# A fourth paired slab in every gate and up group, with hidden tiles split by adding DMAs

## The chip, the cores and the metric

The kernel runs on one core of one Trainium2 chip. The metric is device microseconds from the start to the end of one execution. The median of three runs of the kernel before is 1436.71 us (1436.64 to 1439.13).

The engines are called by their names in the profile: PE multiplies matrices and accumulates into PSUM banks, ACT (ScalarE) casts and applies functions, DVE (VectorE) adds and subtracts, POOL (GpSimd) here issues DMAs of its own queue, SP issues the weight loads.

## The reference

One layer over 256 rows of width 2048: four mixers side by side, a cross attention, and a SwiGLU of width 5632, each behind a norm, with residual sums. All is float32. The part that matters here:

```python
def swiglu(h, w_gate_up, w_down):
    gate, up = jnp.split(h @ w_gate_up, 2, axis=-1)
    return (jax.nn.silu(gate) * up) @ w_down
...
        x = x + swiglu(rms_norm(x, norm_g[l, 2]), w_gate_up[l], w_down[l])
    return rms_norm(x, final_norm_g)
```

## The kernel before

**Two parts per operand.** Every operand of a matrix product is split into a high part, rounded to the short float32 form that PE multiplies in one pass (`fp32r`), and a low part, what the rounding left. A product is three matmuls: high by high, high by low, low by high (`part`, lines 431 to 436). ACT casts the high part of a weight (`wh`), DVE subtracts it from the original to get the low part (`wl`), and PE can multiply by a piece of weight only when both are there.

**The weight stream.** All weights come in the order of use as slabs of 16 blocks of 128x128, 1 MB each, into one of three buffers `raw`. A slab is prepared in halves of up to 1024 columns (`_half`, lines 132 to 138: cast at 135, subtraction at 136). Four pairs of buffers hold prepared halves; `_fill` writes the preparation of a half three halves ahead of its use. A half's cast has to wait until PE has finished with the half four places earlier.

**Ordinary and paired slabs.** In the gate and up product each of ten groups makes 512 columns of gate and 512 of up for both row blocks of 128. Its work is a plan of eight letters, one per slab. An ordinary slab, "N", holds four pieces of 512 columns, each multiplied for two row blocks: 24 matmuls. A paired slab, "S", holds two pieces of gate and two of up for two of the 16 inner tiles; by sums of weights and sums of activations (`combine`, lines 438 to 455, made once, kept in tiles `z`) the same product takes seven parts and not eight: 21 matmuls (`paired_rows`, lines 491 to 505). Its weights are prepared in four halves of 1024, 512, 1024 and 1024 columns (`_sums`, lines 140 to 165: adds at 157, casts at 159, subtractions at 160), which PE uses for 6, 3, 6 and 6 matmuls. The sums overwrite the raw columns: the first add writes columns that the first half reads.

The sums of weights are made in two ways. In a slab of the set `SUMMED` a tile `two` gets a copy of one quarter twice by SP and then two other quarters added on top by an adding DMA on POOL's queue (`_load`, lines 98 to 106); DVE then adds twice. In the other paired slabs, those of the down product, DVE adds four times. `two` has two buffers, and its DMAs are issued when the slab before is loaded.

**The end of a group.** After the third paired slab, `mixed` (line 1064) makes the mixed sums from four PSUM banks with four adds on DVE, `gated` (1073) adds the gate banks and takes the Silu on ACT, and after the eighth slab `upped` (1079) adds the up banks, multiplies by the row gains and the gate, transposes and sends the hidden tiles to memory with two DMAs of POOL.

**Hidden tiles.** The hidden values return turned, as 44 tiles of 128x256 (`fetch`, lines 1087 to 1103): a POOL DMA loads a tile into a temporary, then `split` (289) casts its high part on ACT and subtracts its low part on DVE into a slot `f`. The first 22 come back during the groups, the others at the start of the down product, which reads `f` in two passes.

**Order.** A scheduler orders each engine's instructions from the program, by order of writing among those that are ready in its own reckoning of time; each engine then executes its list in that order. `keep_place` (line 309) ties instructions to their written place. Background work (`Background`) is written between matmuls by due times reckoned from PE's and DVE's work.

Of the kernel before, what the change touches and what calls it, by code (L numbers as in the profile page):

```python
# [13 lines left out]
F32 = mybir.dt.float32  # L14
F32R = mybir.dt.float32r
# [4 lines left out]
ALU = mybir.AluOpType  # L20
# [3 lines left out]
P = 128  # L24
R = 256
D = 2048
KT = D // P
DFF = 5632
# [13 lines left out]
LATE = 12  # L42

GATE_UP = 1920 // 16 + 8
GROUP = "NNSNSNSN"

DOWN = GATE_UP + 80
PASSES = "NNNNSNNSNNSNNSNNSNNSNN", "NSNSNSNSNSNSNSNSNSNNNN"

PAIRED = {a + i for a, plan in [(GATE_UP + 8 * j, GROUP) for j in range(10)] + [(DOWN, PASSES[0]), (DOWN + 22, PASSES[1])]  # L50
          for i, x in enumerate(plan) if x == "S"}
SUMMED = {i for i in PAIRED if i < DOWN}

LAG, OWED, SOON, FAR = 1.3, 0.9, 0.01, 18.0
V_NG = 0
# [16 lines left out]
class Stream:  # L72
# [21 lines left out]
    def _load(self, n):  # L94

        nc = self.nc
        self.raw = self.rawp.tile([P, 2048], F32, name="raw", tag="raw")
        if n // 16 + 1 in SUMMED:
            W, t = self.W[n // 16 + 1], self.sums.tile([P, 1024], F32, name="two", tag="two")
            for a in (0, 512):  # L100
                nc.sync.dma_start(t[:, a:a + 512], W[:, 1536:2048])
            nc.gpsimd.dma_start(t, W[:, 512:1536], accum_op=ALU.add)  # L102
            self.two.append(t)
        if n // 16 in SUMMED:
            nc.sync.dma_start(self.raw[:, 0:1536], self.W[n // 16][:, 0:1536])
            return
        for a, b in zip(CUTS[n], CUTS[n][1:]) if n in CUTS else [(0, 1024), (1024, 2048)] if self.after else [(0, 2048)]:
            (nc.scalar if (n, a) == (0, 0) else nc.sync).dma_start(self.raw[:, a:b], self.W[n // 16][:, a:b])
            if self.after:
                self.after.pop(0)()  # L110

    def _half(self):

        nc, n = self.nc, self.made
        if n % 16 == 0 and self.phase == 0:
            self._load(n)
        if n // 16 in PAIRED:
            return self._sums()
# [86 lines left out]
class Background:  # L205
# [17 lines left out]
    def first(self, g):  # L223

        self.q.sort(key=lambda e: e[0] is not g)
# [29 lines left out]
class Block:  # L255
# [42 lines left out]
    def split2(self, hi, lo, src):  # L298
        self.nc.scalar.copy(hi, src)
        self.tt(lo, src, hi.bitcast(F32), ALU.subtract)  # L300

    def gap(self, pool, n):

        pool.tile([P, n // 4], F32, name=f"gap{next(self.kept)}")
# [159 lines left out]
    def paired_rows(self, w, cols, slots, sums, plan, mixed, first, ready=None, late=0, before=None, swap=False):  # L464

        st, s, nk = self.st, len(sums), len(slots)  # L470
        rest = [k for k in range(nk) if not any(k in ks for ks, _ in sums)]
        steps = [(c, k) for c in range(2) for k in rest]
        todo, q = iter(sums), {}
        count = {"a0": len(rest) + s, "a1": len(rest) + s, "b0": len(rest) + s, "b1": len(rest)}
        left, total = {}, 0

        def put(name, hi, lo, wh, wl):
            if name not in q:
                for x in [name] if name in count else "1675":
                    q[x] = (self.bank if (name in count) == swap else self.gbank)()  # L480
                    left[x] = count.get(x, s)
            new = left[name] == count.get(name, s)
            left[name] -= 1
            self.part(q[name][:, :], hi, lo, wh, wl, new, left[name] == 0)

        form = lambda t, r: (t[:, r * P:(r + 1) * P], t[:, R + r * P:R + (r + 1) * P])
        n = done = 0
        for i, kind in enumerate(plan):
            if before:
                before(i)  # L490
            if kind == "S":
                ks, z = next(todo)
                a = [form(slots[ks[0]], 0), form(slots[ks[1]], 0), form(slots[ks[1]], 1)]
                hi, lo, x4 = self.forms(z, slots[ks[0]])
                x1, s2, s3 = ((hi[:, i * P:i * P + P], lo[:, i * P:i * P + P]) for i in range(3))
                t = (("5", x1), ("7", s3))
                pairs = iter((("1", a[0]), ("b0", x4), ("a0", a[1]), *(t if st.n // 16 in SUMMED else t[::-1]), ("a1", a[2]), ("6", s2)))
                for parts in st.take_sums(w, ks, cols):
                    for wh, wl in parts:
                        name, (hi, lo) = next(pairs)  # L500
                        put(name, hi, lo, wh, wl)
                        self.bg.poll()
                done += 1
# [543 lines left out]
    def gate_up(self, gp, f, z):  # L1047
# [39 lines left out]
        def fetch(k0, k1, ahead, pause, wait=0):  # L1087

            m = {}
            for k in range(k0, k1 + ahead):  # L1090
                if k < k1:
                    while len(stored) <= k // 4:
                        yield
                    m[k] = self.tmp()
                    self.load_turned(m[k], self.ff, k)
                if k >= k0 + ahead:
                    while wait and self.bg.now < stored[(k - ahead) // 4] + wait:
                        yield
                    mark = self.mark()
                    self.split(f[k - ahead], m.pop(k - ahead))  # L1100
                    self.keep_place(mark)
                    self.have = k - ahead + 1
                    yield pause

# [15 lines left out]
                yield 3.0  # L1120
                yield from self.combine(z, *(self.h3[k] for k in ks))

        sums = [((2 * i, 2 * i + 1), z[i]) for i in range(GROUP.count("S"))]
        comb = self.bg.add(combined())
        ps = self.gemm_rows("w_gate_up", [0, DFF], self.h3,
                            parts=[(range(8), [0]), (range(8, 12), [0]), (range(12), [1]), (range(12, 16), [0]), (range(12, 16), [1])],
# [4 lines left out]
        early = self.bg.add(fetch(0, FT - 22, 3, 2.0, 15))  # L1131
        self.bg.drain(comb)
        for j in range(1, DFF // 512):
            upped(j, self.paired_rows("w_gate_up", [j * 512, DFF + j * 512], self.h3, sums, GROUP, mixed, gated, swap=j % 2 == 0)[0])
        self.bg.drain(early)
        self.fetch = self.bg.add(fetch(FT - 22, FT, 6, SOON))

# [73 lines left out]
    def down_end(self, f, ss, ps, rest, split):  # L1211
# [6 lines left out]
        def norm(p, r):  # L1218

            s, y, b, v, a = ss[:, 4 * r + 3:4 * r + 4], *(ss[:, 8 + 4 * r + i:9 + 4 * r + i] for i in range(4))  # L1220
            if r == 0:
                self.tt(self.half(3, 0), self.half(3, 0), p, ALU.add)
                p = self.half(3, 0)
            nc.scalar.activation(self.bank()[:, :], p[:, :], AF.Square, accum_out=s)
            nc.scalar.activation(y, s, AF.Abs_reciprocal_sqrt, scale=1.0 / D, bias=b)
            nc.vector.scalar_tensor_tensor(out=v, in0=s, scalar=1.0 / D, in1=b, op0=ALU.mult, op1=ALU.add)

            nc.vector.scalar_tensor_tensor(out=a, in0=y, scalar=v, in1=y, op0=ALU.mult, op1=ALU.mult)
            nc.vector.scalar_tensor_tensor(out=v, in0=a, scalar=-10.0 / 3, in1=a, op0=ALU.add, op1=ALU.mult)
            nc.vector.scalar_tensor_tensor(out=a, in0=v, scalar=5.0, in1=y, op0=ALU.add, op1=ALU.mult)  # L1230
            for c in range(4):
                x = self.half(c, r)
                if c == 3:
                    nc.vector.scalar_tensor_tensor(out=x, in0=p[:, :], scalar=a, in1=fg[:, 3 * 512:4 * 512], op0=ALU.mult, op1=ALU.mult)
                elif c:
                    nc.scalar.activation(x, x, AF.Copy, scale=a)
                else:
                    nc.vector.tensor_scalar(out=x, in0=x, scalar1=a, scalar2=None, op0=ALU.mult)
                (nc.scalar if c == 1 else nc.sync).dma_start(self.t["out"][r * P:(r + 1) * P, c * 512:(c + 1) * 512], x)

        mark = self.mark()
# [7 lines left out]
        for r in range(2):  # L1249
# [4 lines left out]
            for c in range(3):  # L1254
                x = self.half(c, r)
                self.stt(x, x, 0.375, fg[:, c * 512:(c + 1) * 512], ALU.mult, ALU.mult)
        nc.scalar.mul(fg[:, 3 * 512:4 * 512], fg[:, 3 * 512:4 * 512], 0.375)
        for r in range(2):
            for k, wh, wl in held:
                self.part_rows(ps[r], r, f[k], wh, wl, False, k == FT - 1)  # L1260
            norm(ps[r], r)


# [627 lines left out]
```

## Time and profile before

The profiled execution took 1435.07 us, 1.64 us under the median; its span from first to last instruction is 1433.3 us.

| engine | busy us | share of the span |
|---|---|---|
| PE | 1423.0 | 99% |
| DVE | 1146.2 | 80% |
| ACT | 815.2 | 57% |
| POOL | 234.8 | 16% |

The ten gate and up groups with pairs run from about 778 to 1193 us of the span, the down product from there to the end. A row of the timeline gives start, duration, engine, line, operation, output and inputs, shapes, the count of instructions merged into the row, and in brackets the engine's idle time before it and what ended it. A row of stretches gives the length and then each engine's busy time.

### The profile page before, as it was taken

How to read it: one execution, taken by the hardware profiler on the slowest of the kernel's cores; microseconds unless marked ns; L12 is line 12 of the kernel's file. 1: busy time of each engine (PE TensorE's matmuls, PEld its weight loads, DVE VectorE, ACT ScalarE, POOL GpSimd, SP SyncE). 2: the span in 40 equal slices, each digit the busy share in tenths (PEclk: the TensorE clock that was granted, in tenths of full speed). 3: DMA queues.
4: the chain of work that ended last, by engine and by line, in shares of the span. 5: the costliest groups of instructions: out<-in, count | busy, mean ns of one | idle time of the engine just before them, and what ended most of it. 6: DMA issues, size and time to landing. Idle time of an engine off the chain costs nothing.

```text
span 1433.3 us, 18652 instructions
## 1 busy us (share of the span) xinstructions
PE 1423.0 (99%) x6589; PEld 1180.7 (82%) x6589; DVE 1146.2 (80%) x1738; ACT 815.2 (57%) x1183; POOL 234.8 (16%) x306
## 2 busy tenths in 40 slices
PE   9999999999999999999999999999999999999997
PEld 8888888888888888888888888888888888888886
DVE  6667868777877767777677888898888888989997
ACT  7556565446645555556554656555555556655655
POOL 0000100013212223531431121122011002000000
PEclk9999999999999999999999999999999999999999
DMA  9876564546667788964986999889999887655554
GB/s 352 299 285 248 205 206 162 175 169 224 202 196 236 234 267 252 274 200 166 289 239 209 286 286 277 278 275 282 294 293 288 268 260 229 219 230 179 193 218 147
DMA packets 73037, 343.79 MB, mean 240 GB/s; under 512 B 10957, under 2 KB 12654, under 8 KB 45168
## 3 DMA queue, kind: packets, MB, share of 16 engines
q1 hardware_dynamic: 54848, 288.98, 57.5%
q0 software_dynamic: 17664, 52.97, 15.8%
q8 instruction: 51, 0.84, 0.2%
q10 hardware_dynamic: 432, 0.66, 0.1%
q14 instruction: 42, 0.34, 0.1%
HBM read 322.12 MB, written 20.45 MB: 239 GB/s over the span
## 4 chain that ended last, share of the span: by engine, by line
PE 97%; DVE 1%; ACT 0%; DMA 0%; issue 0%; SPq 0%; ACTq 0%
PE pg L433 22%; PE pg L434 22%; PE pg L435 22%; PE pm L434 7%; PE pm L435 7%; PE pm L433 7%; PE pg L381 4%; PE pg L382 2%; PE pm L1344 1%; PE pm L1022 1%; PE pm L993 1%; DMA raw<-in_W 0%; PE pm L1753 0%; DVE res L283 0%; PE pm L994 0%
## 5 line engine op out<-in xcount | busy, mean ns | idle before, releaser
L136 DVE TENSOR_TENSOR wl<-raw,wh 128x1024 fp32r<-128x1024 f32 (+1 forms) x413 | 494.8, 1212 | 166.1 <-ACT wh L135 163.2
L135 ACT CAST wh<-raw 128x1024 fp32r<-128x1024 f32 (+1 forms) x413 | 424.5, 1043 | 283.9 <-PE pg L435 196.4
L433 PE MATMUL pg<-wh,act 128*128 128x512 f32 (+1 forms) x1191 | 465.6, 391 | 0.0
L434 PE MATMUL pg<-wl,act 128*128 128x512 f32 (+1 forms) x1191 | 463.9, 389 | 0.4 <-DVE wl L136 0.2
L435 PE MATMUL pg<-wh,act 128*128 128x512 f32 (+1 forms) x1191 | 463.9, 389 | 0.0
L433 PEld LDWEIGHTS pg<-wh,act 128*128 128x128 f32 x1191 | 223.8, 188 | 47.8 <-issue 1.5
L434 PEld LDWEIGHTS pg<-wl,act 128*128 128x128 f32 x1191 | 223.8, 188 | 47.2 <-DVE wl L136 1.3
L435 PEld LDWEIGHTS pg<-wh,act 128*128 128x128 f32 x1191 | 223.7, 188 | 47.2 <-DVE act L283 0.4
L159 ACT CAST wh<-raw 128x1024 fp32r<-128x1024 f32 (+1 forms) x150 | 137.0, 921 | 146.8 <-DVE raw L157 46.4
L160 DVE TENSOR_TENSOR wl<-raw,wh 128x1024 fp32r<-128x1024 f32 (+1 forms) x150 | 156.1, 1061 | 57.0 <-ACT wh L159 56.8
L434 PE MATMUL pm<-wl,act 128*128 128x512 f32 x309 | 120.5, 390 | 0.1
L433 PE MATMUL pm<-wh,act 128*128 128x512 f32 x309 | 120.2, 389 | 0.0
L435 PE MATMUL pm<-wh,act 128*128 128x512 f32 x309 | 120.2, 389 | 0.0
L381 PE MATMUL pg<-act,wh 128*128 128x512 f32 x256 | 90.5, 395 | 0.0
L382 PE MATMUL pg<-act,wl 128*128 128x256 f32 x256 | 71.8, 280 | 0.0
L434 PEld LDWEIGHTS pm<-wl,act 128*128 128x128 f32 x309 | 58.0, 188 | 13.0 <-DVE wl L136 0.6
L433 PEld LDWEIGHTS pm<-wh,act 128*128 128x128 f32 x309 | 58.0, 188 | 12.0
L435 PEld LDWEIGHTS pm<-wh,act 128*128 128x128 f32 x309 | 58.0, 188 | 12.0
L102 POOL DMA_DIRECT2D two<-in_W x30 | 26.6, 887 | 241.2 <-DMA two<-in_W 116.0
L157 DVE TENSOR_TENSOR raw<-raw 128x512 f32<-128x512 f32 x90 | 62.0, 689 | 1.3
L159 ACT CAST wh<-two 128x1024 fp32r<-128x1024 f32 x30 | 31.6, 1052 | 51.1 <-PE pg L435 21.7
L381 PEld LDWEIGHTS pg<-act,wh 128*128 128x128 f32 x256 | 48.1, 188 | 10.5
(375 smaller groups left out, 1821.9 us busy)
## 6 DMA issues: line engine op xcount, KB each, us to landing
raw<-in_W SPq DMA_DIRECT2D x216, 1024.0 KB, 5.6
raw<-in_W SPq DMA_DIRECT2D x30, 768.0 KB, 6.1
two<-in_W SPq DMA_DIRECT2D x60, 256.0 KB, 4.9
two<-in_W POOLq DMA_DIRECT2D x30, 512.0 KB, 9.3
raw<-in_W SPq DMA_DIRECT2D x11, 512.0 KB, 7.6
hidden<-g POOLq DMA_DIRECT2D x22, 256.0 KB, 3.7
tmp<-hidden POOLq DMA_DIRECT2D x44, 128.0 KB, 5.4
features<-tmp POOLq DMA_DIRECT2D x32, 128.0 KB, 5.3
```

Source lines behind the costliest of these rows:

```text
L102: nc.gpsimd.dma_start(t, W[:, 512:1536], accum_op=ALU.add)
L135: nc.scalar.copy(wh[:, a:b], r[:, a:b])
L136: nc.vector.tensor_tensor(out=wl[:, a:b], in0=r[:, a:b], in1=wh[:, a:b].bitcast(F32), op=ALU.subtract)
L157: nc.vector.tensor_tensor(out=out, in0=a, in1=b, op=ALU.add)
L159: nc.scalar.copy(wh, src)
L160: nc.vector.tensor_tensor(out=wl, in0=src, in1=wh.bitcast(F32), op=ALU.subtract)
L381: self.nc.tensor.matmul(p[:, :], wh, slot[:, :], start=start, stop=False)
L382: self.nc.tensor.matmul(p[:, 0:R], wl, slot[:, 0:R], start=False, stop=stop)
L433: self.nc.tensor.matmul(p, hi, wh, start=start, stop=False)
L434: self.nc.tensor.matmul(p, hi, wl, start=False, stop=False)
L435: self.nc.tensor.matmul(p, lo, wh, start=False, stop=stop)
L993: nc.tensor.matmul(p[:, :], q[d][:, r * P:(r + 1) * P], kt[d][:, :], start=d == 0, stop=False)
```

## The change

Four things change.

- The plan of a group is "NSNSsNSN" where it was "NNSNSNSN". The fourth paired slab, small "s", is not in `SUMMED`: it is loaded whole and DVE makes all its sums. A fourth combined tile `z3` lies in the pool of the group stage.
- The sums in `two` are loaded two slabs ahead of use where it was one.
- A hidden tile's low part is made in another way: ACT casts the tile a second time with factor -1 into the place of the low part, and an adding DMA on POOL's queue adds the tile to it. The two casts keep their written places.
- PE's matmuls of the paired plans, and those held for the last rows, keep their written places.

```diff
-GROUP = "NNSNSNSN"
+GROUPS = "NSNSsNSN",
...
-          for i, x in enumerate(plan) if x == "S"}
-SUMMED = {i for i in PAIRED if i < DOWN}
+          for i, x in enumerate(plan) if x in "Ss"}
+SUMMED = {GATE_UP + 8 * j + i for j in range(10) for i, x in enumerate(GROUPS[j % len(GROUPS)]) if x == "S"}
...
-        if n // 16 + 1 in SUMMED:
-            W, t = self.W[n // 16 + 1], self.sums.tile([P, 1024], F32, name="two", tag="two")
+        if n // 16 + 2 in SUMMED:
+            W, t = self.W[n // 16 + 2], self.sums.tile([P, 1024], F32, name="two", tag="two")
...
+    def split_far(self, hi, lo, src):
+
+        mark = self.mark()
+        self.nc.scalar.copy(hi, src)
+        self.nc.scalar.mul(lo, src, -1.0)
+        self.keep_place(mark)
+        self.nc.gpsimd.dma_start(lo, src, accum_op=ALU.add)
...
+            mark = self.mark()
             self.part(q[name][:, :], hi, lo, wh, wl, new, left[name] == 0)
+            self.keep_place(mark)
...
-            if kind == "S":
+            if kind in "Ss":
...
-                    mark = self.mark()
-                    self.split(f[k - ahead], m.pop(k - ahead))
-                    self.keep_place(mark)
+                    t = f[k - ahead]
+                    self.split_far(t[:, 0:R], t[:, R:512], m.pop(k - ahead))
...
-        sums = [((2 * i, 2 * i + 1), z[i]) for i in range(GROUP.count("S"))]
+        z = z + [gp.tile([P, 1024], F32R, name="z3")]
+        sums = [((2 * i, 2 * i + 1), z[i]) for i in range(4)]
...
-            upped(j, self.paired_rows("w_gate_up", [j * 512, DFF + j * 512], self.h3, sums, GROUP, mixed, gated, swap=j % 2 == 0)[0])
+            plan = GROUPS[(j - 1) % len(GROUPS)]
+            upped(j, self.paired_rows("w_gate_up", [j * 512, DFF + j * 512], self.h3, sums[:8 - plan.count("N")], plan, mixed, gated,
+                                      swap=j % 2 == 0)[0])
...
         for r in range(2):
+            mark = self.mark()
             for k, wh, wl in held:
                 self.part_rows(ps[r], r, f[k], wh, wl, False, k == FT - 1)
+            self.keep_place(mark)
             norm(ps[r], r)
```

More of the change, by code (lines that the diff above doesn't have):

```diff
@@ L44 @@
 GATE_UP = 1920 // 16 + 8
-GROUP = "NNSNSNSN"
+GROUPS = "NSNSsNSN",
 DOWN = GATE_UP + 80
 PASSES = "NNNNSNNSNNSNNSNNSNNSNN", "NSNSNSNSNSNSNSNSNSNNNN"
-PAIRED = {a + i for a, plan in [(GATE_UP + 8 * j, GROUP) for j in range(10)] + [(DOWN, PASSES[0]), (DOWN + 22, PASSES[1])]
-          for i, x in enumerate(plan) if x == "S"}
-SUMMED = {i for i in PAIRED if i < DOWN}
+PAIRED = {a + i for a, plan in [(GATE_UP + 8 * j, GROUPS[j % len(GROUPS)]) for j in range(10)] + [(DOWN, PASSES[0]), (DOWN + 22, PASSES[1])]
+          for i, x in enumerate(plan) if x in "Ss"}
+SUMMED = {GATE_UP + 8 * j + i for j in range(10) for i, x in enumerate(GROUPS[j % len(GROUPS)]) if x == "S"}
 LAG, OWED, SOON, FAR = 1.3, 0.9, 0.01, 18.0
```

## The prediction

> **What bounds the kernel now.** I read the page first: busy shares, then the slices. Then the busy time by stretches over the gate and up groups, the list of waits, and last the instructions in order of time around one group's end and one paired slab.
>
> ```profile
> span 1433.3 us, 18652 instructions
> PE 1423.0 (99%) x6589; PEld 1180.7 (82%) x6589; DVE 1146.2 (80%) x1738; ACT 815.2 (57%) x1183; POOL 234.8 (16%) x306
> DVE  6667868777877767777677888898888888989997
> ```
>
> TensorE (PE) is never free, so a matmul removed is worth its full time, provided nothing else then ends last. VectorE (DVE) is next: eight or nine tenths in the second half. The stretches (41 us is nearly one group):
>
> ```profile
> core 0: us, PE busy (x) PEld busy (x) DVE busy (x) ACT busy (x) POOL busy (x), PEclk, DMA share, GB/s
> 906.00:947.00 41.00, 40.94 (x180) 33.42 (x179) 36.10 (x45) 23.61 (x29) 7.76 (x9) 1.00 0.90 282
> 1111.00:1152.00 41.00, 41.00 (x182) 33.80 (x181) 35.40 (x41) 23.83 (x28) 4.21 (x5) 1.00 0.90 276
> 1300.00:1400.00 100.00, 100.00 (x443) 82.81 (x442) 96.09 (x138) 58.03 (x74) 0.00 (x0) 1.00 0.56 203
> 1400.00:1433.00 33.00, 24.54 (x108) 19.55 (x106) 23.85 (x50) 15.86 (x29) 0.00 (x0) 0.94 0.45 159
> ```
>
> DVE has 5 to 6 us left in 41. That rest is not free to use: it falls where DVE waits for ScalarE (ACT), which waits until PE gives a weight buffer back.
>
> ```profile
> PE pg L434 <- DVE wl L136: 0.2, 1, 0.2
> ...
> DVE wl L160 <- ACT wh L159: 50.5, 49, 1.7
> ```
>
> PE lost 0.2 us to weights in the whole run; DVE waited 50.5 us in the groups. The cause is the depth of four weight buffers (a "half" each: 12 matmuls in an ordinary slab, but 6, 3, 6, 6 in a paired one). The last half of a paired slab can only be cast when PE frees the buffer four halves back.
>
> **The gain.** PE at the end of one group: paired slab, ordinary slab, next group.
>
> ```profile
> 975.38 0.39 PE L433 MATMUL pm<-wh,act 128*128 128x512 f32 x1
> ...
> 980.14 0.39 PE L433 MATMUL pg<-wh,act 128*128 128x512 f32 x1
> ...
> 985.58 0.39 PE L433 MATMUL pm<-wh,act 128*128 128x512 f32 x1
> ```
>
> A paired slab takes 980.14-975.38 = 4.76 us (21 matmuls), an ordinary one 985.58-980.14 = 5.44 (24): 0.227 us per matmul. One more pair saves 0.68 us per group, 6.8 us in ten.
>
> **What DVE gets for it.** An ordinary slab costs DVE two 128x1024 subtractions. The new "s" slab is not summed by DMA: three 128x1024, one 128x512 and four adds. All of these stand in the second down pass:
>
> ```profile
> 1371.14 1.82 DVE L160 TENSOR_TENSOR wl<-raw,wh 128x1024 fp32r<-128x1024 f32 x2
> 1372.88 2.87 DVE L157 TENSOR_TENSOR raw<-raw 128x512 f32<-128x512 f32 x4
> 1375.66 1.22 DVE L160 TENSOR_TENSOR wl<-raw,wh 128x1024 fp32r<-128x1024 f32 x1
> ```
>
> Start to start, the 1024 with the 512 takes 1.74 us (1.14 and 0.60) and the four adds 2.78. The s slab: 3x1.14+0.60+2.78 = 6.80 us, against PE's 4.76. The ordinary slab it replaces: 2.28. So DVE gets 4.52 us per group, and 35.4 of 41 becomes about 40 in a group of 40.9. Work alone would just fit; with the waits above it does not.
>
> **First place: s directly behind S.** Now the DVE rows around a group's end and the paired slabs after it:
>
> ```profile
> 1151.70 1.22 DVE L136 TENSOR_TENSOR wl<-raw,wh 128x1024 fp32r<-128x1024 f32 x1
> ...
> 1154.63 1.41 DVE L287 SCALAR_TENSOR_TENSOR h<-h,rc,g 128x512 f32<-128x512 f32 x2
> 1155.95 1.30 DVE L557 STREAM_TRANSPOSE g<-h 128x512 f32<-128x512 f32 x2
> 1157.17 1.19 DVE L136 TENSOR_TENSOR wl<-raw,wh 128x1024 fp32r<-128x1024 f32 x1
> 1158.28 1.82 DVE L160 TENSOR_TENSOR wl<-raw,wh 128x1024 fp32r<-128x1024 f32 x2
> 1160.01 0.69 DVE L157 TENSOR_TENSOR raw<-two,raw 128x512 f32<-128x512 f32 x1
> 1161.09 1.23 DVE L160 TENSOR_TENSOR wl<-two,wh 128x1024 fp32r<-128x1024 f32 x1 [0.39 <-ACT wh L159]
> 1162.23 0.68 DVE L157 TENSOR_TENSOR raw<-raw 128x512 f32<-128x512 f32 x1
> 1164.11 1.23 DVE L160 TENSOR_TENSOR wl<-raw,wh 128x1024 fp32r<-128x1024 f32 x1 [1.19 <-ACT wh L159]
> ...
> 1174.01 1.23 DVE L160 TENSOR_TENSOR wl<-raw,wh 128x1024 fp32r<-128x1024 f32 x1 [1.54 <-ACT wh L159]
> 1175.37 2.36 DVE L136 TENSOR_TENSOR wl<-raw,wh 128x1024 fp32r<-128x1024 f32 x2
> ```
>
> ```profile
> 1172.93 1.05 ACT L159 CAST wh<-raw 128x1024 fp32r<-128x1024 f32 x1 [1.72 <-PE pm L435]
> 1174.29 2.00 ACT L135 CAST wh<-raw 128x1024 fp32r<-128x1024 f32 x2 [0.31 <-PE pm L435]
> ```
>
> ```profile
> 1177.44 0.39 PE L433 MATMUL pm<-wh,act 128*128 128x512 f32 x1
> ```
>
> At 1174.01 DVE subtracts the last half of a paired slab, at 1175.37 the first half of the next slab, both just after their casts, which waited for PE: neither can be earlier. PE reaches that next slab at 1177.44. Put s there. Its first add overwrites raw columns that its first half still reads, so no add can go ahead of 1175.37. DVE: first half to 1176.51, second to 1177.11, adds to 1179.89, third half done 1181.12 (1.23 long). PE wants it one matmul into the third half: 1177.44+9x0.227+0.23 = 1179.71. Late by 1.41. The fourth half's cast runs beside, its subtraction is done about 1182.3, wanted at 1181.07+1.41: no more. So 1.4 us in each of ten groups, 14.1.
>
> **Second place: the first pair one slab after the group's end.** DVE's end-of-group work (adds, gains, transposes) ran without a gap until 1157.17. PE began the new group at
>
> ```profile
> 1151.60 0.39 PE L433 MATMUL pm<-wh,act 128*128 128x512 f32 x1
> ```
>
> so 5.57 us later. Today the second ordinary slab covers this. After, PE reaches the paired slab at 1157.04 and its halves at 1158.40, 1159.08 and 1160.45. The piece at 1151.70 becomes that slab's first half. Behind 1157.17 come its second half (0.60), one add (0.60), the half from "two" (1.14) and the other add, the order these rows show when "two" is ready. Third half done: 1157.17+1.20+1.23 = 1159.60, wanted 1159.31, late 0.3. Other add done 1157.17+2.34+0.68 = 1160.19; cast 1.05, subtraction 1.23 and two 0.05 handovers: 1162.57, wanted 1160.67: late 1.9 in all. With both adds ahead of "two" (a day in the other order) it is 1.0. I take 1.9, for the rows after a group's end have that order. Nine groups follow a paired one: 17.1; the first follows a group with four such rows only.
>
> **The other edits.**
> SwiGLU low parts: 22 subtractions leave DVE in the early groups and 22 in the first down pass. The stretch with these (36.10) and one without (35.40) both ran without PE waits, and neither place above holds one, so I credit 0; at best 0.33 us in a few places. ACT gets 44 more casts, 0.40 each, 17.6 us at 57% busy: hidden. POOL gets 44 more issues:
>
> ```profile
> L564 POOL DMA_DIRECT2D tmp<-hidden x44: 884/884/904, 785.9 to 1226.5; - x44
> ...
> two<-in_W POOLq DMA_DIRECT2D x30, 512.0 KB, 9.3
> ...
> values<-tmp POOLq DMA_DIRECT2D x16, 128.0 KB, 2.2
> ...
> 1223.46 0.88 POOL L564 DMA_DIRECT2D tmp<-hidden  x1 [7.27 <-DVE act L283]
> 1225.62 1.76 POOL L564 DMA_DIRECT2D tmp<-hidden  x2 [1.28 <-DVE act L283]
> ...
> 1193.08 0.39 PE L433 MATMUL pg<-wh,f 128*128 128x512 f32 x1
> ```
>
> An adding DMA of 128 KB has no row; a plain one lands in 2.2 us, an adding one four times its size in 9.3. Down starts at 1193.08; its last hidden tile is wanted seven ordinary and two paired slabs and three steps of 1.36 later: 1193.08+38.1+9.5+4.1 = 1244.8. Its load is out by 1227.4 and lands about 5.4 later; with two casts, one issue and 9.3 it is whole by 1244. Covered, but narrowly: 0, or up to 9.3 if the queue holds it up. On the same queue a weight add can stand behind four hidden adds (a load's 5.4 plus 0.9 each); issuing it two slabs ahead adds 4.8 to 5.4 of slack, so 0. SP issues no more than before and the s slab loads 1 MB as the slab it replaces did; the hidden adds put 0.5 MB per group on some 11.6 (41 us at 282 GB/s): 0. The fourth combination falls in the first group, where DVE idles: 0. Kept places fix an order and issue nothing.
>
> **Sum**, against this execution's 1435.07 us (span 1433.3): -6.8+14.1+17.1 = +24.4, that is 1459.5. The median of the three runs stands 1.6 higher, so **1461 us**. Its own range runs from 1.0 at each place (-6.8+10+9, 1447) to 1472, when order adds half a subtraction to each.
>
> **Rivals.**
> *Faster.* The stall at both places is nothing, since VectorE has caught up by then: 1435.07-6.8 = 1428 (1430 at the median). For it: the second down pass alternates ordinary and unsummed paired slabs with DVE at 96.09 of 100 and PE at 100.00. Against it: there an ordinary slab, with 3.2 us to spare on DVE, stands ahead of each. It decides if lateness stays under 0.36 us at each of 19 places. 0.09. *Within 0.2%:* 0.04.
> *One place only.* If the scheduler draws the group's first paired slab ahead of gains and transposes (2.5 us of DVE), only s stalls: 1435.07-6.8+14.1 = 1442. Against it: 1151 to 1157 shows the opposite. 0.14.
> *Larger stalls by order.* Where a half is late, a ready half of the next slab may be put ahead of it on DVE, 1.14 us each: 19x1.14 = 21.7 more, 1482. For it: adds and halves already swap places in the rows. 0.16.
> *Late hidden tiles:* 9.3 more, 1470. 0.04.
> *The clock falls.* In the last stretch PE idled 8.46 of 33 us and the granted clock was 0.94, 2 us lost. If every stop after a group's end cost that: nine more times 2, 1479. The Trainium skill ("TensorE: Matmul & The Clock Gate", "Why this matters for your kernels") says only idle gaps beyond about 3 us bring the half-rate clock back; by that rule my stops, at most 1.9, keep the clock and the sum stands. No run here yet shows stops of that length. 0.03.
> The forecast keeps 0.50.
>
> **Numbers.** A difference under 0.2% (2.9 us) can't be told from none here. Leaving out faster and same (0.13) and the upper tip of the order rival gives 1441 to 1479. Faster 0.09, same 0.04, slower 0.87.
>
> **What would show it.** PE's matmuls fall by 30. The waits should list PE behind "wl" L160 with some 20 to 35 us, where it had 0.2; in each group one pause in the third half of s and one in the third or fourth half of the first pair. Group starts should lie about 44 us apart, not 41.6. I am wrong if PE still waits for nothing, or if it waits for hidden tiles or for "raw".

## The result and the profile after

The changed kernel takes 1536.99 us (median of five runs, 1533.58 to 1539.28), the kernel before beside it 1436.64 (1435.42 to 1439.13): a ratio of 1.0697 with a 95% interval of 1.0678 to 1.0716, slower. The profiled execution has a span of 1535.0 us, 101.7 more than before. The page of the changed kernel (busy time, and two rows of the 40 slices):

```profile
span 1535.0 us, 18725 instructions
PE 1450.3 (94%) x6559; PEld 1179.3 (77%) x6559; DVE 1178.3 (77%) x1762; ACT 846.8 (55%) x1249; POOL 274.0 (18%) x350
PE   9999999999999999999999999999999947799997
PEclk9999999999999999999999999999999968999998
```

The 30 matmuls are gone (6589 before). TensorE now stops, and four fifths along (slice 33 of 40, from 1228 us), where the groups end, it is down to four tenths for a slice and its granted clock falls. What it waited for, from the list of waits (engine, line, released by: us in total, times, longest):

```profile
PE pg L443 <- DMA f<-tmp: 18.3, 2, 14.9
PE pm L442 <- DVE wl L160: 12.4, 15, 0.9
PE pg L442 <- DVE wl L160: 11.1, 14, 0.9
PE pg L443 <- DMA act<-tmp: 10.2, 6, 3.0
PE pg L441 <- ACT f L305: 7.3, 1, 7.3
PE pg L443 <- DMA z<-tmp: 4.4, 1, 4.4
PE pm L441 <- ACT wh L159: 2.9, 6, 0.6
```

Lines 441 to 443 are the three matmuls of `part`: high by high, high by low weights, low by high weights. L160 makes the low weights, L305 and L308 are the first cast and the adding DMA of `split_far`. So there are two main kinds of wait: for low weights (L442, 23.5 us), and for hidden tiles, which before had none: 32.9 us for their low parts (L443, "DMA f", "act" and "z") and one stop of 7.3 for a high part (L441, "ACT f L305"). By stretches (span; PE, PEld, DVE, ACT and POOL busy; granted clock, DMA share, GB/s):

```profile
906.00:947.00 41.00, 37.95 (x161) 29.61 (x160) 37.47 (x45) 22.05 (x25) 4.19 (x5) 1.00 0.81 241
1111.00:1152.00 41.00, 39.37 (x169) 31.30 (x168) 34.95 (x43) 20.91 (x23) 3.75 (x5) 1.00 0.83 257
1240.00:1280.00 40.00, 18.70 (x62) 13.80 (x62) 6.95 (x7) 16.98 (x39) 36.98 (x42) 0.67 0.94 195
1340.00:1440.00 100.00, 100.00 (x442) 82.64 (x441) 90.86 (x136) 56.60 (x75) 0.84 (x1) 1.00 0.54 194
```

In the groups TensorE is short by 1.6 to 3.1 us of 41; in the 40 us behind the last group it gets through 62 matmuls instead of some 176, while GpSimd (POOL), busy 4 of 41 in the groups, is busy 36.98 of 40. The second down pass is untouched.

Adding up every distance between two matmul starts beyond the usual 0.227 us (those of 0.03 us and more) gives 46.2 us between 790 and 1231 (the groups), 55.8 between 1231 and 1350 (the start of down) and 5.9 behind it (all of it at the end); before had 1.9 from 790 to its end. Less that and 6.8 for the removed matmuls it is the difference, but for some 3 us, mostly of smaller distances.

### The profile page after: what moved, and what is told of

It reads as the page before. It is cut to its first block, busy times and chain, and to the rows that moved or that the text cites. A ratio compares the mean times of both kernels' runs of the same rounds, so it can differ in the third digit from the quotient of the medians.

```text
span 1535.0 us, 18725 instructions
## 1 busy us (share of the span) xinstructions
PE 1450.3 (94%) x6559; PEld 1179.3 (77%) x6559; DVE 1178.3 (77%) x1762; ACT 846.8 (55%) x1249; POOL 274.0 (18%) x350
## 4 chain that ended last, share of the span: by engine, by line
PE 83%; DVE 7%; DMA 3%; ACT 3%; issue 2%; POOL 1%; SPq 0%; ACTq 0%; POOLq 0%
PE pg L442 19%; PE pg L443 19%; PE pg L441 18%; PE pm L442 6%; PE pm L443 6%; PE pm L441 5%; PE pg L389 4%; DVE wl L160 3%; PE pg L390 2%; DVE raw L157 2%; DVE wl L136 2%; DMA tmp<-hidden 1%; PE pm L1358 1%; DMA raw<-in_W 1%; ACT wh L135 1%
## 5 line engine op out<-in xcount | busy, mean ns | idle before, releaser
L136 DVE TENSOR_TENSOR wl<-raw,wh 128x1024 fp32r<-128x1024 f32 (+1 forms) x393 | 472.0, 1212 | 191.6 <-ACT wh L135 189.8
L135 ACT CAST wh<-raw 128x1024 fp32r<-128x1024 f32 (+1 forms) x393 | 405.8, 1042 | 273.5 <-PE pg L443 192.2
L443 PE MATMUL pg<-wh,act 128*128 128x512 f32 (+1 forms) x1166 | 456.1, 391 | 10.8 <-DMA act<-tmp 10.2
L442 PE MATMUL pg<-wl,act 128*128 128x512 f32 (+1 forms) x1166 | 456.2, 391 | 6.7 <-DVE wl L160 6.5
L441 PE MATMUL pg<-wh,act 128*128 128x512 f32 (+1 forms) x1166 | 457.3, 392 | 4.9 <-ACT act L299 2.4
L159 ACT CAST wh<-raw 128x1024 fp32r<-128x1024 f32 (+1 forms) x190 | 174.6, 924 | 190.2 <-PE pg L443 87.7
L443 PEld LDWEIGHTS pg<-wh,act 128*128 128x128 f32 x1166 | 219.2, 188 | 60.3 <-DMA act<-tmp 13.2
L442 PEld LDWEIGHTS pg<-wl,act 128*128 128x128 f32 x1166 | 219.5, 188 | 56.4 <-DVE wl L160 10.2
L441 PEld LDWEIGHTS pg<-wh,act 128*128 128x128 f32 x1166 | 219.5, 188 | 54.1 <-ACT wh L159 3.6
L160 DVE TENSOR_TENSOR wl<-raw,wh 128x1024 fp32r<-128x1024 f32 (+1 forms) x190 | 199.0, 1063 | 69.5 <-ACT wh L159 69.2
L442 PE MATMUL pm<-wl,act 128*128 128x512 f32 x284 | 112.7, 397 | 7.7 <-DVE wl L160 7.7
L441 PE MATMUL pm<-wh,act 128*128 128x512 f32 x284 | 112.1, 395 | 2.3 <-ACT wh L159 2.3
L443 PE MATMUL pm<-wh,act 128*128 128x512 f32 x284 | 111.6, 393 | 0.0
L157 DVE TENSOR_TENSOR raw<-raw 128x512 f32<-128x512 f32 x130 | 89.4, 687 | 2.5
L442 PEld LDWEIGHTS pm<-wl,act 128*128 128x128 f32 x284 | 53.9, 190 | 22.6 <-DVE wl L160 11.5
L441 PEld LDWEIGHTS pm<-wh,act 128*128 128x128 f32 x284 | 53.9, 190 | 15.7 <-ACT wh L159 4.5
L443 PEld LDWEIGHTS pm<-wh,act 128*128 128x128 f32 x284 | 53.9, 190 | 11.0
L574 POOL DMA_DIRECT2D tmp<-hidden x44 | 53.3, 1417 | 17.8 <-DMA act<-tmp 6.1
```

The lines of the kernel that those rows point to most:

```text
L135: nc.scalar.copy(wh[:, a:b], r[:, a:b])
L136: nc.vector.tensor_tensor(out=wl[:, a:b], in0=r[:, a:b], in1=wh[:, a:b].bitcast(F32), op=ALU.subtract)
L157: nc.vector.tensor_tensor(out=out, in0=a, in1=b, op=ALU.add)
L159: nc.scalar.copy(wh, src)
L160: nc.vector.tensor_tensor(out=wl, in0=src, in1=wh.bitcast(F32), op=ALU.subtract)
L441: self.nc.tensor.matmul(p, hi, wh, start=start, stop=False)
```

## The experiments

All times are medians; each batch is set against its own runs of the kernel before, 1435.8 to 1437.1, so differences across batches are good to about 1 us. All runs also combine the fourth pair of tiles. In short, with the ratio and its interval:

| run | what it is | us | ratio |
|---|---|---|---|
| two_ahead | before + weight adds two slabs ahead | 1437.0 | 1.0002 (0.9993 to 1.0011) |
| old_plan | + the kept places | 1443.8 | 1.0052 (1.0034 to 1.0070) |
| early_far | + adding DMAs for the 22 early tiles | 1452.7 | 1.0112 (1.0098 to 1.0126) |
| three_pairs | + adding DMAs for all 44 | 1474.2 | 1.0257 (1.0236 to 1.0277) |
| false_debt | + 6 us a group in the reckoning only | 1499.1 | 1.0436 (1.0421 to 1.0452) |
| best_four | before + adds two slabs ahead, fourth pair, early tiles not held back | 1465.5 | 1.0197 (1.0182 to 1.0212) |
| undebted_near | + the kept places | 1493.5 | 1.0393 (1.0378 to 1.0409) |
| subtracted | + early tiles held back by the reckoning | 1499.5 | 1.0440 (1.0425 to 1.0456) |
| the change | + adding DMAs for all 44 | 1537.0 | 1.0697 (1.0678 to 1.0716) |

The upper five keep the old plan NNSNSNSN, the lower four have the new one; within each part every row adds one thing to the row above it.

### The planner's debt

A step of the prediction took the first 22 hidden tiles to come back during the groups. They don't. GpSimd's rows of the changed kernel (start, length, line, what, and in brackets the idle time ahead and what ended it):

```profile
793.33 0.85 POOL L308 DMA_DIRECT2D act<-tmp  x1 [3.98 <-ACT act L306]
...
1234.32 0.85 POOL L308 DMA_DIRECT2D act<-tmp  x1 [31.36 <-ACT act L305]
...
1244.78 3.55 POOL L308 DMA_DIRECT2D f<-tmp  x2
```

One adding DMA at 793.33, the next at 1234.32. (Twelve loads are drawn ahead into the first three groups, at 785 to 880; eleven of these tiles then sit unsplit in the eleven `tmp` places.) The code says why: `poll` (lines 241 to 244) steps background work only while `owed`, the VectorE work that the planner has reckoned and TensorE has not yet worked off, is under 0.9. By its own formula (elements/960 + 0.155 an operation) a group owed 37.7 us before against 41.5 of TensorE; with the unsummed pair it owes 42.3 against 40.8. By this reckoning the debt grows by 1.5 us from group to group, and the early tiles wait until they are drained behind the last one.

```diff
 # undebted
-            if self.owed < OWED and self.now >= e[1]:
+            if (self.owed < OWED or e[0] is self.free) and self.now >= e[1]:
...
-            e[1] = self.now + self.owed + (w or LAG)
+            e[1] = self.now + (0.0 if e[0] is self.free else self.owed) + (w or LAG)
...
+        self.bg.free = early
 # subtracted
-                    self.split_far(t[:, 0:R], t[:, R:512], m.pop(k - ahead))
+                    mark = self.mark()
+                    self.split(t, m.pop(k - ahead))
+                    self.keep_place(mark)
 # three_pairs
-GROUPS = "NSNSsNSN",
+GROUPS = "NNSNSNSN",
 # false_debt: as three_pairs, and in upped()
+            self.bg.dve(0, 39)
```

> Changed kernel, but the early return of the hidden tiles is stepped by its due times alone and no longer held back by the planner's reckoned VectorE debt. Debt theory (with an unsummed fourth pair the planner reckons more VectorE work than TensorE time in every group, its debt never falls under 0.9, so the early 22 tiles are not returned until the groups are over): the pauses at the start of the down passes, 56 us, fall under 10, the 46 us of pauses in the groups stay; 1481 to 1491. Rival (the adding DMAs on GpSimd's queue are slow wherever they stand): pauses at the start of down stay above 30, over 1505.

> Changed kernel, but the hidden tiles' low parts by VectorE subtractions as before; everything else of the change stays. Debt theory: the 22 early tiles still come all at once behind the last group, at 1 to 1.4 us of GpSimd issue per load, and TensorE waits for the first dozen of them: 20 to 35 of the 56 us stay, 1502 to 1517, with the rest of the 56 due to the adding DMAs behind the loads on GpSimd. Rival (adding DMAs slow in themselves): under 5 of the 56 us stay, 1481 to 1487. A second rival (late tiles alone, whatever makes the low part): above 1530.

> Changed kernel with the old plan of slabs NNSNSNSN (three summed pairs), so low parts by adding DMAs, weight adds two slabs ahead and kept places stay. Debt theory: reckoned VectorE work per group is under TensorE's time, the early tiles return during the groups as before, no pauses: 1433 to 1440, as the kernel before. Rival (adding DMAs slow wherever they stand): TensorE waits for hidden tiles at the start of down, 1450 or more.

> The three-pair plan with the rest of the change, and 6 us of VectorE work per group put into the planner's reckoning that does not exist (no instruction is added). Debt theory: the early hidden tiles come back only after the last group and TensorE waits for them at the start of down as in the changed kernel, 45 to 60 us, with no pause in the groups: 1481 to 1496. Rival (the reckoning does not matter, only real VectorE work does): as the three-pair kernel without it, 1433 to 1440.

Measured: 1523.7 (ratio 1.0602, 1.0579 to 1.0624), 1499.5, 1474.2 and 1499.1. Neither theory alone holds: undebted and three_pairs took the time of the rival, subtracted lies between the two ranges, and false_debt 3 us above the debt theory's. The false debt costs 24.9 us beside the same kernel without it, and not an instruction was added; the pauses at the start of down rise from 23.7 to 58.4, those in the groups fall from 12.5 to 0.4, and its waits repeat those of the changed kernel:

```profile
PE pg L443 <- DMA f<-tmp: 17.7, 2, 14.9
PE pg L443 <- DMA act<-tmp: 12.4, 4, 6.9
PE pg L441 <- ACT f L305: 7.3, 1, 7.3
```

So the debt is real. But three_pairs, whose early tiles do come back in the groups, is still 37.6 us slower than before (6.8 of it for the kept places, below): the adding DMAs cost wherever they stand. And freeing the early tiles in the changed kernel gained only 13.3: by the distances between matmul starts the pauses at the start of down fell from 55.8 to 29.3, while in the groups they grew from 46.2 to 62.3, for there the tiles' casts and adding DMAs now stood.

### The price of the adding DMAs, and of the kept places

```diff
 # old_plan: three_pairs with the subtractions of "subtracted"
 # two_ahead: old_plan without the newly kept places
-            mark = self.mark()
             self.part(q[name][:, :], hi, lo, wh, wl, new, left[name] == 0)
-            self.keep_place(mark)
...
-            mark = self.mark()
             for k, wh, wl in held:
                 self.part_rows(ps[r], r, f[k], wh, wl, False, k == FT - 1)
-            self.keep_place(mark)
 # early_far: old_plan, in fetch()
+                    if k0 == 0:
+                        self.split_far(t[:, 0:R], t[:, R:512], m.pop(k - ahead))
 # lead: three_pairs
-            while self.have < min(FT, k + 3):
+            while self.have < min(FT, k + 8):
 # plain_copy: three_pairs
-        self.nc.gpsimd.dma_start(lo, src, accum_op=ALU.add)
+        self.nc.gpsimd.dma_start(lo, src)
```

> Old plan of slabs NNSNSNSN and low parts by VectorE subtractions: of the change only the weight adds two slabs ahead and the kept places stay (and a fourth pair of tiles is combined for nothing). If they cost nothing, as the false-debt run suggests (no pause in its groups): 1434 to 1440. Rival (issuing the weight adds a slab earlier takes DMA time from the raw weights): over 1445, with ScalarE waiting for raw clearly more than before's 30 us.

> The old-plan kernel (low parts by subtractions) without the two newly kept places (the paired steps' matmuls, and the last held matmuls), so of the change only the weight adds two slabs ahead stay. If the kept places cost the 7.6 us that the old-plan kernel is slower than before (TensorE stopped 3.0 us at the identity matmuls behind the last pass, which before had matmuls put ahead of them, then ran eight matmuls at half clock; and 2.2 us at 1234): 1434 to 1440. Rival (the earlier weight adds cost it): 1441 or more.

> The old-plan kernel with adding DMAs for the low parts of the 22 early hidden tiles alone; the 22 late ones stay with VectorE subtractions. DMA-time theory (the adding DMAs in the groups, where the DMA engines were already 0.92 busy, make the raw weights land late): 8 to 12 us of pauses in the groups stay and the 17 to 20 at the start of down go, 1451 to 1457. Rival (all that the adding DMAs cost comes from the late tiles at the start of down): 1443 to 1446.

> The three-pair kernel (adding DMAs for all 44 tiles), but in the down pass a hidden tile is asked for eight tiles ahead of its use instead of three (10.9 us instead of 4.1). Due-time theory (an adding DMA takes 4 to 12 us to land behind 1 to 3 us of issue, and three tiles are too short a lead): the 20 us of pauses at the start of down fall under 8, 1458 to 1465. Rival (the rate of GpSimd's queue, of the DMA engines, or of the eleven shared tmp tiles limits, not the lead): 1470 to 1478.

> The three-pair kernel with the 44 adding DMAs as plain DMAs of the same tiles to the same places (the subtraction of the low part is left out, so the low part holds the tile itself). If it is the adding that makes them long (a second source is read): landing falls from 12.8 us in the groups and 4.3 in down to under 5 and 3, pauses shrink by half, 1452 to 1463. Rival (rows of 1 KB from one on-chip place to another cost the same whether added or not): 1468 to 1478.

**Kept places.** old_plan 1443.8, two_ahead 1437.0 beside 1436.6: weight adds two slabs ahead cost nothing, the kept places 6.8 us under the old plan (old_plan itself fell between its two ranges). TensorE's rows behind the last pass, first of before, then of old_plan:

```profile
1408.35 0.28 PE L1244 MATMUL pm<-tmp,identr 128*128 128x256 f32 x1
1408.46 0.39 PE L433 MATMUL pm<-wh,act 128*128 128x512 f32 x1
...
1409.96 0.28 PE L1244 MATMUL pm<-tmp,identr 128*128 128x256 f32 x1
```

```profile
1411.56 0.39 PE L443 MATMUL pm<-wh,act 128*128 128x512 f32 x1
1412.88 0.39 PE L1258 MATMUL pm<-tmp,identr 128*128 128x256 f32 x1 [0.93 <-ACT tmp L299]
1414.39 0.38 PE L1258 MATMUL pm<-tmp,identr 128*128 128x256 f32 x1 [1.13 <-DVE tmp L283]
1415.26 0.84 PE L1258 MATMUL pm<-tmp,identr 128*128 128x256 f32 x2 [0.49 <-ACT tmp L299]
...
1416.90 0.63 PE L441 MATMUL pm<-wh,act 128*128 128x512 f32 x1
```

Before, ordinary matmuls stand between the identity matmuls and fill the time until the next split is ready. With places kept, each identity matmul is waited for with ready work behind it, and the matmuls after that run 0.43 apart instead of 0.227.

**Early adding DMAs.** early_far is 8.9 us above old_plan. What ScalarE waited for between 800 and 1060, old_plan and then early_far:

```profile
ACT wh L135 <- DMA raw<-in_W: 13.4, 5, 4.6
```

```profile
ACT wh L135 <- DMA raw<-in_W: 27.8, 12, 5.8
```

The DMA engines were 0.93 busy in these 260 us and became 0.94, and yet the waits for raw weights doubled; the median from issue to landing of a 1024 KB slab between 800 and 1190 went from 6.8 to 8.7 us (7.4 in the kernel before), and that of the adding DMAs into f tiles was 13.0. Here, with the DMA engines 0.93 busy, half a megabyte a group was not free. As plain copies of all 44 tiles, which leave the subtraction out (1462.1, 1.0165, 1.0145 to 1.0186), the same transfers cost 12 us less than added; of the pauses in the groups 4.2 of 12.5 us stay, and at the start of down 18.1 of 23.7. Counted in pauses, the adding makes most of the early price and a quarter of the late one. How it does so isn't shown: the time came into the range expected, but the landing in the groups, expected under 5 us, was 12.0 beside 12.8.

**Late adding DMAs.** three_pairs is 21.5 us above early_far. A lead of eight tiles instead of three (1469.1, 1.0225, 1.0206 to 1.0245) gains 5 and falls between its two ranges; 19.4 of the 23.7 us of pauses stay, so the lead is not the main limit. Rows of three_pairs, VectorE, ScalarE and GpSimd:

```profile
1246.27 0.29 DVE L283 TENSOR_TENSOR tmp<-tmp 128x128 f32<-128x128 f32 x1 [3.42 <-DMA act<-tmp]
...
1250.72 0.82 DVE L283 TENSOR_TENSOR tmp<-tmp 128x128 f32<-128x128 f32 x3 [4.16 <-DMA act<-tmp]
```

```profile
1251.05 0.30 ACT L299 CAST y<-tmp 128x128 fp32r<-128x128 f32 x1 [9.09 <-DVE tmp L283]
```

```profile
1251.52 2.72 POOL L574 DMA_DIRECT2D tmp<-hidden  x3 [8.41 <-DVE tmp L283]
```

The waiting VectorE operations belong to `combine`; they read and write only "tmp" tiles. They wait for an adding DMA because that DMA still reads the tmp tile they are to overwrite: all draw on the same eleven. ScalarE stands behind them with a cast, and the next three loads on GpSimd too. A subtraction reads its tmp tile for some 0.4 us; an adding DMA holds it until it has landed (4.3 us median here). Giving these tiles places of their own wasn't tried, so that this makes the late price is read from the rows and not shown by a run.

### The two places, and the fourth pair by itself

```diff
 # second_place: "subtracted" with
+GROUPS = "NSNSNNSN",
 # first_place: "subtracted" with
+GROUPS = "NNSsNNSN",
 # undebted_near: the edits of undebted and of subtracted
 # unkept: the change without the newly kept places (as in two_ahead)
 # best_four: undebted_near without the newly kept places
 # nn_four, nsns, nn_two: best_four with
+GROUPS = "NNSNsSNN",
+GROUPS = "NSNSNSNS",
+GROUPS = "NNsSNSSN",
```

> Three summed pairs at NSNSNNSN, so only the first pair moves to one slab behind the group's end; low parts by VectorE subtractions, so that no adding DMA of hidden tiles disturbs. Forecast's step (1.9 us in each of nine groups; 2.0 measured in the changed kernel's groups): 1453 to 1457, group starts 43.5 us apart. Rival (the pauses there come from VectorE being loaded by the fourth pair, not from the place): 1440 or less. The planner's debt stays paid, so no hidden tile is late in either.

> Three pairs at NNSsNNSN, the second unsummed and directly behind the first; the first pair stays two slabs behind the group's end; low parts by VectorE subtractions. Forecast's step: 1.4 us in each of ten groups, 1451; with the order seen in the changed kernel (a ready half of the next slab put ahead), 2.2: 1459. Rival (adjacency is harmless with two ordinary slabs on either side): 1440 or less.

> Four pairs as changed, low parts by VectorE subtractions, and the early return of hidden tiles not held back by the reckoned debt. If late tiles and adding DMAs make up all that lies beyond the weights' pauses: before's time less 6.8 for the removed matmuls plus 42 to 46 of pauses in the groups, 1472 to 1477. Rival (the 22 subtractions put back on a full VectorE lengthen the groups further): 1480 or more.

> The changed kernel without its two newly kept places. If they cost in it what they cost under the old plan (5 us behind the last pass, and some 2 us at the start of down that late tiles may cover): 1527 to 1533, with no pause at the identity matmuls at the end. Rival (an effect of the old plan alone): 1535 or more.

> The changed plan NSNSsNSN with all else mended: low parts by VectorE subtractions, early tiles not held back by the debt, no newly kept places; the fourth pair and the weight adds two slabs ahead stay. The fourth pair's own price: the run with kept places, 1493.5, less 5 to 8 for them, 1485 to 1489. Rival (pauses that the kept places caused inside the groups go too): 1475 or less.

> As the kernel with all else mended, but the four pairs at NNSNsSNN: two ordinary slabs behind each group's end, the unsummed pair behind an ordinary slab, a summed one directly behind it. Place theory: only the adjacency is left, 2.2 to 2.6 us in each of ten groups, less 6.8 for the removed matmuls: 1452 to 1456. Rival (with the unsummed pair behind an ordinary slab VectorE keeps up and nothing stalls): 1429 to 1436, faster than before.

> As the kernel with all else mended, but four summed pairs at NSNSNSNS: none directly behind another, the first one slab behind the group's end, which a pair now ends. Place theory: 2.0 to 3.0 us in each of nine groups, less 6.8: 1448 to 1457, and the adds of a group's end, now all behind the last pair, may lengthen that. Rival (VectorE's whole work is the bound, wherever the pairs stand, as the reckoning of 42 against 41 us says): as the changed order mended, 1475 or more.

> As the kernel with all else mended, but four pairs at NNsSNSSN: two ordinary slabs behind the group's end, then two adjacent couples. (The plan NNSNsSNN of the run before this one holds only three pairs; its unsummed pair ahead of a summed one cost some 0.5 us a group.) Place theory: no stall behind the group's end, two couples at 0.5 to 1.4 us in each of ten groups, less 6.8: 1440 to 1458. Rival (VectorE's total work is the bound in any order of four pairs): 1465 or more. Under 1434 it would be the first order of four pairs that pays.

second_place takes 1471.2 (1.0236, 1.0219 to 1.0253), first_place 1468.8 (1.0225, 1.0209 to 1.0242). Beside old_plan, 27.4 and 25.0 us for one moved pair each (in first_place that pair is unsummed too), 3.0 and 2.5 a group. Both places are real, without a fourth pair, and both dearer than expected.

undebted_near, 1493.5, is where its rival put it: with 22 tiles returned in the groups (each a load, a cast and a subtraction) the pauses there grow from 45.3 (subtracted) to 56.9, and those at the start of down fall from 19.3 to 4.4. About half of that growth is clock and not stops: at five places the matmuls behind a stop start 0.43 us apart and not 0.227 (half clock), which adds up to some 7 us where subtracted lost under 2. best_four fell to its rival too: 28.0 us less without the kept places, four times their price under the old plan; these half-clock stretches are gone with them. In the changed kernel itself (unkept, 1512.6, 1.0530, 1.0514 to 1.0546) they cost 24.4, again more than expected: 17 of it are pauses in the groups (46.2 to 29.2), 4.5 at the end. TensorE in a late half of unkept:

```profile
1024.27 0.73 PE L441 MATMUL pg<-wh,z 128*128 128x512 f32 x2
1025.22 0.73 PE L441 MATMUL pm<-wh,act 128*128 128x512 f32 x2 [0.21 <-ACT wh L135]
1025.79 0.42 PE L442 MATMUL pg<-wl,z 128*128 128x512 f32 x1
```

Four matmuls that need only high weights go ahead of the first that needs low ones. (The front part says that TensorE can multiply by a piece only when both of its parts are there; the first of the three matmuls needs the high part alone.) With places kept each L442 follows its own L441, and TensorE stands still for the subtraction.

So the fourth pair by itself is best_four (with the adds two slabs ahead, and early tiles free of the debt): 1465.5, 28.5 above its batch's runs of before, that is 35.3 us of pauses less 6.8 of matmuls. Its two stretches:

```profile
906.00:947.00 41.00, 38.70 (x164) 29.79 (x163) 37.85 (x48) 21.94 (x28) 7.77 (x9) 1.00 0.86 264
1111.00:1152.00 41.00, 38.37 (x162) 29.62 (x161) 37.50 (x45) 22.87 (x26) 5.12 (x6) 1.00 0.83 259
```

VectorE is 37.5 to 37.9 of 41 busy, up from 35.4 to 36.1 before. All pauses in the groups, 32.5 us, lie at the two places of the forecast: ten at the first, 10.4 us together, and nine at the second, 22.1 (each counted with the lengthened matmuls behind it).

nn_four can't tell place from total work, for NNSNsSNN holds only three pairs. It shows one thing: an unsummed pair ahead of a summed one, behind an ordinary slab and without kept places, costs 5 us in all (1442.1, 1.0031, 1.0019 to 1.0044). The real other orders of four came out dearer than best_four's: nn_two 1480.6 (1.0312, 1.0295 to 1.0329) and nsns 1490.3 (1.0364, 1.0348 to 1.0381). Place theory expected 1440 to 1458; both times are where its rival, VectorE's total work, put them. The two stretches of nsns speak against that rival all the same:

```profile
906.00:947.00 41.00, 37.74 (x157) 29.50 (x156) 34.34 (x43) 22.12 (x27) 8.39 (x10) 0.96 0.92 272
1111.00:1152.00 41.00, 38.13 (x154) 30.26 (x154) 32.37 (x35) 22.18 (x24) 8.00 (x10) 0.92 0.95 275
```

VectorE is less busy there than before (32.4 to 34.3 of 41). TensorE stops nine times, 27.2 us in all, for a low half of the pair one slab behind a group's end, while VectorE does the group's last adds, gains and transposes first, and some 11 us are lost to matmuls 0.43 us apart. How much of the fourth pair's price in the other orders goes with its places and how much with VectorE's and the DMA engines' total work stays open; that no order of four tried comes near 1436 is what the runs show. Nothing tried beats the kernel before.

## Why the prediction was wrong

The direction was right and its main mechanism is there; the size was not: 1459.5 forecast for a profiled execution, and 1536.8 found. Where the 77 lie: 15 more of pauses in the groups (46.2 against 31.2), 55.8 at the start of down (against 0), 5 more at the end. Its signs came, 30 matmuls fewer and 23.5 us of waits for "wl" L160, and so did one sign of being wrong, waits for hidden tiles.

**The gain** (30 matmuls, 6.8 us): right.

**What DVE gets for it**: right. Its busy time rose by 32.1 us (1146.2 to 1178.3); ten times 4.52 less 44 subtractions of 0.33 is 30.7, and the fourth combination comes on top. That the subtractions taken off earn nothing was wrong with a fourth pair in the groups: returning 22 tiles there with theirs, some 7 us of VectorE, made 11.6 of pauses in undebted_near. What the loads and casts of these tiles have in that isn't told apart.

**First place**: forecast 1.4 a group, "the fourth half's cast runs beside ... no more". Measured, in the changed kernel, TensorE and VectorE:

```profile
1076.89 0.50 PE L441 MATMUL pm<-wh,z 128*128 128x512 f32 x1
1078.32 0.50 PE L442 MATMUL pm<-wl,z 128*128 128x512 f32 x1 [0.93 <-DVE wl L160]
...
1080.59 0.50 PE L442 MATMUL pg<-wl,act 128*128 128x512 f32 x1 [0.60 <-DVE wl L160]
```

```profile
1077.05 1.22 DVE L160 TENSOR_TENSOR wl<-raw,wh 128x1024 fp32r<-128x1024 f32 x1
1078.18 1.22 DVE L136 TENSOR_TENSOR wl<-raw,wh 128x1024 fp32r<-128x1024 f32 x1
1079.32 1.22 DVE L160 TENSOR_TENSOR wl<-raw,wh 128x1024 fp32r<-128x1024 f32 x1
```

The distances are 0.25, 1.20 and 0.76 too long: 2.2. The third half behaves as forecast; then the ready half of the next slab (L136 at 1078.18) is put ahead of the fourth (1079.32). That is the rival of larger stalls by order, here at one place of two.

**Second place**: forecast 1.9; 0.17, 0.63 and 1.22 were found at every group from 829 to 1200, 2.0. Right in the changed kernel; alone, in second_place, 3.0, with one or two ready halves put ahead and some 0.5 of it at half clock.

Together that is 4.2 a group, 40 of the 46.2 in the groups; the rest is 0.11 at the matmul behind each stop and one stretch at half clock. Group starts lie 45.9 us apart, not 44 (hidden stores from 826.92 to 1194.32, eight groups).

**The other edits** is the step that failed. It gave 0, or up to 9.3, to what costs 37.5 (adding DMAs, change beside subtracted), 6.0 (debt, subtracted beside undebted_near) and 28.0 (kept places, undebted_near beside best_four, some 7 of it at half clock). The shares depend on the order in which they are taken: with adding DMAs the debt costs 24.9, under the old plan the kept places 6.8. Three sentences of it fall:
- "whole by 1244" took the early 22 tiles as back by then. The rule that holds them back stands in the code named in the front part; the reckoning above needs no chip.
- "0.5 MB per group on some 11.6 ... : 0" went by bytes. The rows of stretches said that the DMA engines were 0.90 busy, and time was what the weights lacked.
- "Kept places fix an order and issue nothing." They cost no instruction, but take from TensorE the work it would do while it waits. The sums for both places assumed the kept order without saying so.

Two slabs ahead and the fourth combination: 0, as forecast (two_ahead).

**The rivals.** Late hidden tiles came true, at six times its price (55.8 against 9.3): it had only the last tile late, not all of them at once. The clock rival came true in part, below: the half clock came back, in the changed kernel above all behind the groups (granted clock 0.67 between 1240 and 1280). That the forecast, 1461, lies near best_four's 1465.5 does not save its split, and is luck: best_four has no kept order and keeps the subtractions, and its two places cost 10.4 and 22.1 where the forecast had 14.1 and 17.1.

## What to carry to other kernels

Before costing a move of background work at nothing, read the rule that admits it, and redo its arithmetic with the change in: a reckoned resource that goes from under to over its limit doesn't slow the work a little, it shuts it out until the next drain. Cost a transfer by the DMA engines' busy share and by how long it holds its source buffer, not by its bytes alone. And fixing an order can cost every wait that reordering used to hide: look whether ready matmuls of another buffer stood in for late ones.

## What the runs showed of the hardware

Half clock comes after short stops too. In the changed kernel at one place of the groups (TensorE, then the stretch with its granted clock, 0.52):

```profile
892.92 0.50 PE L441 MATMUL pm<-wh,z 128*128 128x512 f32 x1 [0.57 <-ACT wh L159]
894.35 0.49 PE L442 MATMUL pm<-wl,z 128*128 128x512 f32 x1 [0.93 <-DVE wl L160]
...
897.64 0.63 PE L441 MATMUL pm<-wh,z 128*128 128x512 f32 x1
```

```profile
896.00:899.00 3.00, 2.72 (x7) 1.91 (x7) 2.84 (x3) 1.00 (x1) 0.00 (x0) 0.52 0.91 169
```

No stop there is over 0.93 us, and matmuls start 0.43 apart for some 3 us. The other places with 0.25, 1.20 and 0.76 kept the clock; here the first was 0.73. Behind old_plan's identity matmuls, stops of 0.93, 1.13 and 0.49 within 4 us did the same. The prediction drew on the Trainium skill ("TensorE: Matmul & The Clock Gate", section "Why this matters for your kernels"), by which gaps beyond some 3 us bring the half clock back; these rows show it behind shorter ones. Nor does the sum of stops within a few us decide: in undebted_near distances 0.51, 0.42 and 1.64 too long within 4 us kept the clock at 833 (granted 1.00 from 830 to 838) and the same three lost it at 879 (granted 0.50 from 880 to 883.3). What decides, no run here isolates.

An adding DMA of 128 KB from one on-chip tile to another took 4.3 us to land at the start of down and 12.8 in the groups (medians of the act and of the f tiles in three_pairs), a plain copy 2.8 and 12.0: most of the time in the groups is not the adding's. A load of 128 KB on the same queue landed there in 7.2 and 6.9, so the full DMA engines (0.94 and 0.95 busy) hardly explain it alone.
